# Weight buffers divided anew (eight raw, seven high, six low) and an instruction order worked out for loads that land later, in a two-layer hybrid attention block

## The chip, the cores and the metric

The kernel runs on one core of one Trainium2 chip. The metric is device time in microseconds of the whole program, and the time of the kernel before is the median of three runs. One more execution was profiled; every row below is of that one.

## The reference, cut to what matters

The reference runs a layer twice on x (256 tokens, width 1024), each time with weights of its own:

```python
def hybrid_layer(x, ...):
    hn = rms_norm(x, ln1)
    proj = hn @ w_in                      # 1024 x 2824: q, k, v of three mixers, and gates
    ...                                   # MoBA (6 heads), mLSTM (4 heads), sliding window (6 heads)
    x = x + jnp.concatenate([y_moba, y_mlstm, y_swa], axis=-1) @ w_out
    u = rms_norm(x, ln2) @ w_up           # 1024 x 4096
    return x + jnp.square(jax.nn.relu(u)) @ w_down
```

All of it is in float32. The small tensors of a layer (norm gains, convolution weights, sinks, gate biases) come to the kernel as one table per layer.

## The kernel before, in words

**Number format.** To keep float32 accuracy, the kernel splits each weight and each activation into a high and a low part and multiplies three times: high by high, high by low, low by high (`three`, L796; its matmuls are L798, L799 and L800). A split (`split`, L295) is one ScalarE copy that rounds to the high part (it shows as ACT L273, `whi<-raw`) and one VectorE subtraction for the low part (DVE L280, `wlo<-raw,whi`).

**How weights travel.** All weights are cut into units of at most 1040 columns by 128 rows (some 512 KB). A unit goes through three sets of buffers. `load_units` (L499) takes a raw buffer, and SyncE's queue loads the unit into it (SPq L300); it goes through the units strictly in the order of a list, so a load that waits for a buffer holds all later ones. `split_units` (L547) takes one high and one low buffer for each unit, again in the order of a list, and splits the raw one into them. TensorE reads the high and the low buffer; `used` (L334) gives them back after the last matmul. Before the change there are six raw, eight high and seven low buffers (`RAW`, `WHI`, `WLO`, L306 to L308).

**Stages of a layer.** The projections go through w_in in pieces of two or four row blocks, with attention (`pair`, `head`, `mlstm_pair`) between them. Then eight units of w_out are multiplied by four `mix` threads (L1387), each for 128 tokens and 512 columns, and each over all eight units; a unit is given back after the fourth. Then comes the feed-forward stage: 32 units of w_up (`up`, L1440: 24 matmuls of 256 columns each) and 32 row blocks of w_down, taken in pairs (`DownPair`, L368). Of a pair, sums of its quarters are made first: ScalarE copies a quarter out of the raw buffer (`first_sum`, L417), a DMA that adds in flight, issued on POOL (L422), adds another quarter to it, and VectorE makes the other sums (`first_sums`, `sums`, L397 and L426; DVE L280 on `arena` and `mids`). The pair then makes four parts, which `split_units` splits too, and `product` (L1482) multiplies them in seven products of three 512-column matmuls each. The sums need the raw buffers of both row blocks, so these are held longer than those of w_up. Meanwhile ScalarE and VectorE also square the results of `up` (`squared`, L1457) and split them (`fh`, `fl`).

**What sets the order.** Each engine executes its instructions in the order in which the program has them. That order is not written by hand: `Scheduler.run` (L165) simulates the engines while the program is built. Every step of every thread is an `Op` with an estimated duration; the scheduler takes the operation that can start first, and among nearly equal ones that of the lowest rank. For a DMA it adds the bytes at 330 GB/s, a latency of 2.2 us, and, from 60 us of its own clock on, `BUSY` = 0.8 us (L229):

```python
LATENCY = {"PE": 0.20, "ACT": 0.145, "DVE": 0.13, "POOL": 0.15, "DMA": 2.2}
...
            th.step(end + LATENCY[eng] + (BUSY if eng == "DMA" and end > 60 else 0))
```

These estimates decide only the order; on the chip, semaphores make each instruction wait until its inputs are really there. An operation whose input comes later than estimated therefore holds up everything behind it on its engine.

**The next layer's table.** `small_loads` (L648), a thread of rank 81 for layer 1, waits for the last use of layer 0's table (one tile holds both, L598), loads the table of the second layer (279 KB), and has VectorE make eight products from it, the rotary tables with the norm gains (`cg`, `sg`, L659), and `nsink`. The products are needed only in layer 1.

Of the kernel before, what the change touches and what calls it, by code (L numbers as in the profile page):

```python
# [11 lines left out]
F32R = mybir.dt.float32r  # L12
# [19 lines left out]
UNIT = 1040  # L32
# [96 lines left out]
LATENCY = {"PE": 0.20, "ACT": 0.145, "DVE": 0.13, "POOL": 0.15, "DMA": 2.2}  # L129
ISSUE = {"PE": 0.235, "ACT": 0.0, "DVE": 0.0, "POOL": 0.0, "DMA": 0.0}  # L130
SWITCH = 0.2
BUSY = 0.8
URGENTLY = -25
SOON = {"PE": 0.08, "ACT": 0.2, "DVE": 0.05, "POOL": 0.0, "DMA": 0.0}


class Scheduler:
# [27 lines left out]
    def run(self):  # L165
        while self.threads:
# [38 lines left out]
            if best is None:  # L205
                if not self.threads:
# [4 lines left out]
            t0, eng = best[0], best[1].engine  # L211
            t, th, op = min((c for c in ready if c[2].engine == eng and c[0] <= t0 + SOON[eng]),
                            key=lambda c: c[1].rank())
            if eng in ("ACT", "DVE") and op.cost > 0.3 and th.rank() > URGENTLY:

                soon = [c for c in ready if c[2].engine == eng and c[1].rank() <= URGENTLY
                        and t < c[0] < min(t + 0.3, t + op.cost - 0.3)]
# [9 lines left out]
            if op.bank:  # L227
                self.banks[op.bank] = eng, end + LATENCY[eng]
            th.step(end + LATENCY[eng] + (BUSY if eng == "DMA" and end > 60 else 0))  # L229

# [19 lines left out]
def tile_hybrid_block(ctx: ExitStack, tc: tile.TileContext, x, xT, smalls, w_in, w_out, w_up,  # L250
# [12 lines left out]
    def buffers(name, n, shape, dt=F32, pool=None):  # L263
        return Buffers([(pool or sb).tile(shape, dt, name=f"{name}{i}") for i in range(n)], name)
# [10 lines left out]
    def dve(waits, n, fn, rate=0.00104, pointers=(), bank=None):  # L275
        p = sum(isinstance(s, bass.AP) for s in pointers)
        return Op("DVE", n * rate + 0.068 + 0.065 * p, waits, fn, bank)
# [4 lines left out]
    def ts(waits, o, i, s1, s2, op0, op1=None, rate=0.00052):  # L282
        kw = {} if op1 is None else {"op1": op1}
        return dve(waits, free_size(o), lambda: V.tensor_scalar(o, i, s1, s2, op0=op0, **kw), rate, (s1, s2),
                   bank_of(i))
# [13 lines left out]
    def dma(waits, nbytes, o, i, eng=None):  # L299
        return Op("DMA", nbytes / 330e3, waits, lambda: (eng or nc.sync).dma_start(o, i))  # L300
# [2 lines left out]
    TMP = buffers("tmp", 5, [128, 512])  # L303
    mids = sb.tile([128, 10 * 384], F32, name="mids")
    MID = Buffers([mids[:, i * 384:i * 384 + 384] for i in range(10)], "mid")
    RAW = buffers("raw", 6, [128, UNIT])  # L306
    WHI = buffers("whi", 8, [128, UNIT], F32R)
    WLO = buffers("wlo", 7, [128, UNIT], F32R)  # L308
    FH = buffers("fh", 4, [128, 1024], F32R)
    FL = buffers("fl", 4, [128, 1024], F32R)  # L310

# [13 lines left out]
    class Unit:  # L325
# [7 lines left out]
        def used(self, t):  # L333
            self.uses -= 1  # L334
            in_use[0] = max(in_use[0], self.k + 1)
            if self.uses == 0:
                WHI.put(self.ih, t)
                WLO.put(self.il, t)

# [28 lines left out]
    class DownPair:  # L368
# [20 lines left out]
        def read(self, i, t):  # L389
# [4 lines left out]
            if not self.raws[i]:  # L394
                RAW.put(u.ir, u.t)

# [102 lines left out]
    def load_units():  # L499
        for k, u in enumerate(units):  # L500
# [9 lines left out]
            if k == 7:  # L510
                t = yield dma([], 262144, masks_t, masks)
                made.signal(t)
            u.ir, t = yield Get(RAW)
            u.raw = RAW.tiles[u.ir]
            dst = u.raw[:, :u.n].rearrange("p (k c) -> p k c", k=u.nk)
# [31 lines left out]
    def split_units():  # L547
        for k, u in enumerate(splits):
            u.k = k
            whole = isinstance(u, Part)  # L550
            yield Wait(*(u.ready if whole else [u.there]))
            u.ih, th = yield Get(WHI)
            u.il, tl = yield Get(WLO)
            h, lo = WHI.tiles[u.ih], WLO.tiles[u.il]
            raw = u.src() if whole else u.raw[:, :u.n]
# [8 lines left out]
            else:  # L564
                RAW.put(u.ir, t)
                u.hi = h[:, :u.n].rearrange("p (k c) -> p k c", k=u.nk)
# [33 lines left out]
    def table(l, a=0, b=T_END):  # L600
        return tab[l][:, a:b], smalls[l, :, a:b]
# [42 lines left out]
    tab_ev = [Event() for _ in range(DEPTH)]  # L644
# [3 lines left out]
    def small_loads(l, after):  # L648


        yield Wait(*after)
        if l:
            t = yield dma([], 300e3, *table(l))
            tab_ev[l].signal(t)
        g = tab[l][:, T_GB:T_SINK].rearrange("p (s i d) -> p s i d", s=2, i=4)
        t = max(e.t for e in (*after, tab_ev[l]))
        for k, o in enumerate((cg, sg)):
            for i in range(4):
                t = yield dve([t], 128, lambda k=k, o=o, i=i: V.scalar_tensor_tensor(  # L659
                    o[:, i], rope_t[:, k], -1.0 if i % 2 else HD ** -0.5,  # L660
                    g[:, k, i, None, :].to_broadcast([128, 2, HD]), op0=OP.mult, op1=OP.mult))
        t = yield ts([t], nsink, tab[l][:, T_SINK:T_BIAS], -1.0, None, OP.mult)
        small_ev[l].signal(t)
# [244 lines left out]
    class Layer:  # L908
# [703 lines left out]
        def start(self, base):  # L1612
# [59 lines left out]
            if l + 1 < DEPTH:  # L1672
                h2 = [e for b in range(2) for e in self.h2[b]]
                add(81, small_loads(l + 1, h2))
# [17 lines left out]
    sch.add(-9, load_units())  # L1692
    sch.add(50, split_units())
    sch.add(5, small_loads(0, x_ev[1]))
    L = None
    for l in range(DEPTH):
# [75 lines left out]
```

## Time and profile before

| what | us |
|---|---|
| median of three runs | 583.48 (582.37 to 585.88) |
| the profiled execution, its own time | 586.18 |
| its span, first to last instruction | 584.4 |
| TensorE busy in the span | 572.6 (98%) |
| VectorE busy | 541.9 (93%) |
| ScalarE busy | 433.7 (74%) |

How to read it: matmuls overlap, and their recorded ends are modelled, so a TensorE that shows as busy can still have waited; the time between the starts of two matmuls that follow each other tells. A number in brackets behind a row of the timeline is how long the engine stood idle before that row, and who ended it.

### The profile page before, as it was taken

How to read it: one execution, taken by the hardware profiler on the slowest of the kernel's cores; microseconds unless marked ns; L12 is line 12 of the kernel's file. 1: busy time of each engine (PE TensorE's matmuls, PEld its weight loads, DVE VectorE, ACT ScalarE, POOL GpSimd, SP SyncE). 2: the span in 40 equal slices, each digit the busy share in tenths (PEclk: the TensorE clock that was granted, in tenths of full speed). 3: DMA queues.
4: the chain of work that ended last, by engine and by line, in shares of the span. 5: the costliest groups of instructions: out<-in, count | busy, mean ns of one | idle time of the engine just before them, and what ended most of it. 6: DMA issues, size and time to landing. Idle time of an engine off the chain costs nothing.

```text
span 584.4 us, 10665 instructions
## 1 busy us (share of the span) xinstructions
PE 572.6 (98%) x3853; PEld 512.3 (88%) x3853; DVE 541.9 (93%) x1125; ACT 433.7 (74%) x835; POOL 34.3 (6%) x46
## 2 busy tenths in 40 slices
PE   8999999999999999999999999999999999999996
PEld 7999987798889999898689999877999898999884
DVE  6899999689899999999999999977999999999995
ACT  6966898676788776787676768967787786886860
POOL 4000000000010100101000000000100010100110
PEclk9999999999999999999999999999999999999999
DMA  9938346364877867776856353544767777777751
GB/s 317 356 92 229 102 135 190 110 208 120 248 222 206 265 193 234 227 214 190 262 153 175 96 186 109 169 157 144 204 175 237 231 191 216 243 207 227 230 113 72
DMA packets 45285, 111.83 MB, mean 191 GB/s; under 512 B 4048, under 2 KB 17616, under 8 KB 45232
## 3 DMA queue, kind: packets, MB, share of 16 engines
q1 hardware_dynamic: 40208, 102.21, 53.8%
q0 software_dynamic: 4736, 8.79, 9.7%
q8 instruction: 30, 0.49, 0.3%
q14 instruction: 23, 0.19, 0.1%
q10 hardware_dynamic: 288, 0.15, 0.1%
HBM read 110.08 MB, written 1.05 MB: 190 GB/s over the span
## 4 chain that ended last, share of the span: by engine, by line
PE 76%; DVE 9%; DMA 7%; ACT 3%; issue 3%; SPq 0%; DVEq 0%; ACTq 0%
PE ps L798 22%; PE ps L800 22%; PE ps L799 22%; DVE wlo L280 5%; DMA raw<-in_w_down_dram 4%; PE ps L875 2%; PE ps L1311 2%; PE ps L1329 2%; DVE arena L280 2%; PE ps L1500 1%; ACT whi L273 1%; DMA xs<-in_x_dram 1%; ACT arena L273 1%; DMA tab<-in_smalls_dram 1%; DVE xs L289 1%
## 5 line engine op out<-in xcount | busy, mean ns | idle before, releaser
L280 DVE TENSOR_TENSOR wlo<-raw,whi 128x512 fp32r<-128x512 f32 (+3 forms) x236 | 211.2, 916 | 8.1 <-ACT whi L273 7.2
L273 ACT ACTIVATE whi<-raw 128x512 fp32r<-128x512 f32 (+3 forms) x236 | 180.0, 807 | 1.7 <-DMA raw<-in_w_in_dram 1.5
L800 PE MATMUL ps<-hT,wlo 128*128 128x256 f32 x576 | 162.4, 282 | 3.2 <-DVE wlo L280 3.0
L798 PE MATMUL ps<-hT,whi 128*128 128x256 f32 x576 | 162.6, 282 | 0.8 <-ACT arena L273 0.4
L799 PE MATMUL ps<-lT,whi 128*128 128x256 f32 x576 | 161.8, 281 | 0.4 <-DVE lT L289 0.4
L798 PE MATMUL ps<-whi,fh 128*128 128x512 f32 x274 | 113.5, 414 | 0.0
L800 PEld LDWEIGHTS ps<-hT,wlo 128*128 128x128 f32 x576 | 108.7, 189 | 4.5 <-DVE wlo L280 4.5
L798 PEld LDWEIGHTS ps<-hT,whi 128*128 128x128 f32 x576 | 108.6, 189 | 2.8 <-ACT arena L273 0.8
L799 PEld LDWEIGHTS ps<-lT,whi 128*128 128x128 f32 x576 | 108.6, 189 | 1.8 <-DVE lT L289 0.6
L800 PE MATMUL ps<-whi,fl 128*128 128x512 f32 x274 | 107.8, 393 | 0.0
L799 PE MATMUL ps<-wlo,fh 128*128 128x512 f32 x274 | 107.7, 393 | 0.0
L798 PE MATMUL ps<-whi,hT 128*128 128x256 f32 (+2 forms) x256 | 80.2, 313 | 0.6 <-ACT whi L273 0.6
L799 PE MATMUL ps<-wlo,hT 128*128 128x256 f32 (+2 forms) x256 | 76.6, 299 | 0.6 <-DVE wlo L280 0.6
L800 PE MATMUL ps<-whi,lT 128*128 128x256 f32 (+2 forms) x256 | 76.3, 298 | 0.0
L798 PEld LDWEIGHTS ps<-whi,fh 128*128 128x128 f32 x274 | 51.5, 188 | 12.6 <-issue 3.3
L800 PEld LDWEIGHTS ps<-whi,fl 128*128 128x128 f32 x274 | 51.5, 188 | 11.9
L799 PEld LDWEIGHTS ps<-wlo,fh 128*128 128x128 f32 x274 | 51.6, 188 | 11.3 <-issue 2.2
L798 PEld LDWEIGHTS ps<-whi,hT 128*128 128x128 f32 x256 | 49.0, 191 | 3.3 <-issue 1.6
L799 PEld LDWEIGHTS ps<-wlo,hT 128*128 128x128 f32 x256 | 49.1, 192 | 1.6 <-DVE wlo L280 1.1
L800 PEld LDWEIGHTS ps<-whi,lT 128*128 128x128 f32 x256 | 48.9, 191 | 0.0
L273 ACT ACTIVATE arena<-ps 128x512 f32<-128x512 f32 (+3 forms) x52 | 26.2, 508 | 29.8 <-PE ps L800 27.5
L273 ACT ACTIVATE fh<-arena 128x1024 fp32r<-128x1024 f32 x30 | 31.8, 1059 | 16.6 <-DVE arena L280 15.5
(153 smaller groups left out, 816.4 us busy)
## 6 DMA issues: line engine op xcount, KB each, us to landing
raw<-in_w_up_dram SPq DMA_DIRECT2D x64, 512.0 KB, 4.7
raw<-in_w_down_dram SPq DMA_DIRECT2D x64, 512.0 KB, 4.6
raw<-in_w_in_dram SPq DMA_DIRECT2D x24, 512.0 KB, 4.6
raw<-in_w_out_dram SPq DMA_DIRECT2D x16, 512.0 KB, 3.4
raw<-in_w_in_dram SPq DMA_DIRECT2D x16, 384.0 KB, 3.7
arena<-in_w_down_dram POOLq DMA_DIRECT2D x20, 256.0 KB, 4.3
raw<-in_w_in_dram SPq DMA_DIRECT2D x7, 520.0 KB, 6.4
mids<-in_w_down_dram POOLq DMA_DIRECT2D x12, 256.0 KB, 4.3
```

Source lines behind the costliest of these rows:

```text
L273: lambda: A.activation(o, i, func, **kw), bank)
L280: return dve(waits, free_size(o), lambda: V.tensor_tensor(o, a, b, op=op), bank=bank_of(a, b))
L289: lambda: V.scalar_tensor_tensor(o, a, s, b, op0=op0, op1=op1), pointers=(s,),
L798: T.matmul(ps, s[0], m[0], start=start, stop=False)
L799: T.matmul(ps, s[0], m[1], start=False, stop=False)
L800: T.matmul(ps, s[1], m[0], start=False, stop=stop)
L875: T.transpose(ps[:, cs], src[:, cs], ident)
L1311: T.matmul(PS.tiles[ip][:, o], qT[b, i, q], kT[b, kc, k], start=o.start == 0, stop=o.start > 0)
L1329: T.matmul(yps[64 * n:64 * n + 64, o], vv[blk][:, d:d + HD], MID.tiles[pT[h]][:, cols], start=blk == 0, stop=blk == 1)
L1500: T.matmul(ps[:, c:d], self.rT[k][1][:, b], part.f[:, cols], start=k == 0, stop=end and d == 512)
```

## The change

The raw buffers become eight, the high ones seven and the low ones six; their sum stays 21, and all have the same size. `BUSY` goes from 0.8 to 1.5, so the scheduler believes that every load after 60 us of its clock lands 0.7 us later than it did. `LATER`, new, adds another 2.5 us to the time at which it believes the second layer's table to be there. No instruction is added or removed; which buffer each uses, and the order on each engine, follow from the scheduler's run with these numbers.

```diff
@@ -129,8 +129,9 @@
-BUSY = 0.8
+BUSY = 1.5
 URGENTLY = -25
+LATER = 2.5
@@ -303,9 +304,9 @@
-    RAW = buffers("raw", 6, [128, UNIT])
-    WHI = buffers("whi", 8, [128, UNIT], F32R)
-    WLO = buffers("wlo", 7, [128, UNIT], F32R)
+    RAW = buffers("raw", 8, [128, UNIT])
+    WHI = buffers("whi", 7, [128, UNIT], F32R)
+    WLO = buffers("wlo", 6, [128, UNIT], F32R)
@@ -651,7 +652,7 @@
             t = yield dma([], 300e3, *table(l))
-            tab_ev[l].signal(t)
+            tab_ev[l].signal(t + LATER)
```

## Rows read from the trace of the kernel before

**Rows 1.** The page's head and its first part.
```profile
span 584.4 us, 10665 instructions
...
PE 572.6 (98%) x3853; PEld 512.3 (88%) x3853; DVE 541.9 (93%) x1125; ACT 433.7 (74%) x835; POOL 34.3 (6%) x46
```

**Rows 2.** Sums by stretch (PE, PEld, DVE, ACT, POOL; clock, DMA), both feed-forward stages.
```profile
125.00:285.00 160.00, 157.15 (x1030) 142.71 (x1029) 151.95 (x209) 118.64 (x150) 13.11 (x16) 1.00 0.75 221
...
413.00:570.00 157.00, 155.89 (x1034) 142.31 (x1033) 151.18 (x200) 118.10 (x148) 12.90 (x15) 1.00 0.73 208
```

**Rows 3.** Timeline of TensorE: neighbouring matmuls with a late start, layer 0.
```profile
142.27 0.28 PE L799 MATMUL ps<-lT,whi 128*128 128x256 f32 x1
143.99 0.39 PE L800 MATMUL ps<-hT,wlo 128*128 128x256 f32 x1 [1.44 <-DVE wlo L280]
...
152.02 0.39 PE L800 MATMUL ps<-whi,fl 128*128 128x512 f32 x1
152.81 0.39 PE L798 MATMUL ps<-hT,whi 128*128 128x256 f32 x1 [0.40 <-ACT arena L273]
...
164.87 0.28 PE L798 MATMUL ps<-hT,whi 128*128 128x256 f32 x1
164.99 0.28 PE L799 MATMUL ps<-lT,whi 128*128 128x256 f32 x1
165.85 0.39 PE L800 MATMUL ps<-hT,wlo 128*128 128x256 f32 x1 [0.58 <-DVE wlo L280]
```

**Rows 4.** The same of layer 1.
```profile
490.07 0.40 PE L799 MATMUL ps<-wlo,fh 128*128 128x512 f32 x1
490.31 0.39 PE L800 MATMUL ps<-whi,fl 128*128 128x512 f32 x1
491.05 0.38 PE L798 MATMUL ps<-hT,whi 128*128 128x256 f32 x1 [0.35 <-ACT whi L273]
491.27 0.28 PE L799 MATMUL ps<-lT,whi 128*128 128x256 f32 x1
492.31 0.39 PE L800 MATMUL ps<-hT,wlo 128*128 128x256 f32 x1 [0.76 <-DVE wlo L280]
```

**Rows 5.** The chain that ended last (start, duration): the second layer's table.
```profile
124.59 6.30 DMA tab<-in_smalls_dram
```

**Rows 6.** Timeline of VectorE: the first product made from that table.
```profile
130.92 0.29 DVE L659 SCALAR_TENSOR_TENSOR cg<-rope_t,tab 128x128 f32<-128x128 f32 x1 [2.25 <-DMA tab<-in_smalls_dram]
```

**Rows 7.** Waits of SyncE's queue, feed-forward of layer 0 (in total, times, longest).
```profile
SPq L300 <- DVE wlo L280: 99.0, 49, 10.4
```

**Rows 8.** Timeline of ScalarE: copies of a w_down quarter, layers 0 and 1.
```profile
151.64 0.63 ACT L273 ACTIVATE mids<-raw 128x512 f32<-128x512 f32 x1 [2.55 <-DMA raw<-in_w_down_dram]
...
488.26 0.63 ACT L273 ACTIVATE arena<-raw 128x512 f32<-128x512 f32 x1 [3.62 <-DMA raw<-in_w_down_dram]
```

**Rows 9.** Waits of VectorE, feed-forward of layer 0 and, below the dots, of layer 1.
```profile
DVE arena L280 <- ACT arena L273: 3.6, 6, 1.3
DVE mids L280 <- DMA raw<-in_w_down_dram: 0.8, 2, 0.7
...
DVE arena L280 <- ACT arena L273: 3.1, 6, 1.1
DVE arena L280 <- DMA raw<-in_w_down_dram: 1.2, 2, 0.8
```

**Rows 10.** Timeline of VectorE, layer 1: low parts of w_out units, the first, seventh and eighth.
```profile
372.11 1.22 DVE L280 TENSOR_TENSOR wlo<-raw,whi 128x1024 fp32r<-128x1024 f32 x1
...
386.27 1.20 DVE L280 TENSOR_TENSOR wlo<-raw,whi 128x1024 fp32r<-128x1024 f32 x1
...
399.22 2.36 DVE L280 TENSOR_TENSOR wlo<-raw,whi 128x1024 fp32r<-128x1024 f32 x2 [3.16 <-ACT whi L273]
```

**Rows 11.** Timeline of TensorE there: `mix`, seventh unit's first read, fourth thread's first unit.
```profile
393.65 0.40 PE L799 MATMUL ps<-wlo,fh 128*128 128x512 f32 x1
...
397.79 0.40 PE L799 MATMUL ps<-wlo,fh 128*128 128x512 f32 x1
```

## The prediction

> **What bounds the kernel now.** I read the page's first part, then the sums by stage, then TensorE's timeline, and only then the waits. The page shows TensorE busy for 98% of the span and VectorE for 93% [rows 1]. The sums by stage say where that is tight: in the two feed-forward stages, 160 and 157 us long, TensorE is busy for 157.15 and 155.89 us, and VectorE for 151.95 and 151.18, that is 95 and 96% [rows 2]. Two engines are nearly full there, and VectorE feeds TensorE. The clock is 1.00 throughout, so it plays no part.
>
> Since recorded ends of matmuls are modelled, I go by starts. Where nothing is missing, a 256-column matmul starts 0.12 us after the one before it (164.87 to 164.99 [rows 3]), and one after a 512-column matmul 0.24 us (490.07 to 490.31 [rows 4]). What exceeds this is waiting. In layer 0: 143.99 - 142.27 - 0.12 = 1.60, 152.81 - 152.02 - 0.24 = 0.55, 165.85 - 164.99 - 0.12 = 0.74, together 2.89 us [rows 3]. In layer 1: 0.74 - 0.24 = 0.50 and 1.04 - 0.12 = 0.92, together 1.42 us [rows 4]. These five hold 4.31 us; the timeline has three more in layer 0, all under 0.4 us, which I don't count. Whatever a better order may do, it has little more than 4.3 us of TensorE's waiting to take in these stages; the matmuls stay as they are.
>
> Two causes lie behind them. First, the second layer's table is issued at 124.59 and takes 6.30 us [rows 5]; VectorE's next instruction in order is made from it, and so VectorE stands for 2.25 us in mid-stage [rows 6], though layer 1 is far away. The chain that ended last goes from this landing on through VectorE, almost without a break, until 143; the 1.60 us at 143.99 come out of it. Second, raw buffers: in layer 0's stage SyncE waits 99.0 us in 49 waits for VectorE to finish with a raw buffer [rows 7], so each load starts only when the sixth-last unit is done with. ScalarE, which copies a quarter of a w_down row block, arrives before its load: 2.55 us of standing at 151.64, 3.62 at 488.26 [rows 8]. VectorE's sums wait for these copies: 3.6 us in six waits in layer 0 and 3.1 in layer 1, with 0.8 and 1.2 us straight for the load [rows 9]. An engine that is 95% busy doesn't catch up quickly; TensorE's waits at 152.81, 165.85, 491.05 and 492.31 follow such a stand.
>
> **The change part by part.** No instruction comes or goes, so every term is a wait or a shift.
>
> *Table, `LATER` and `BUSY`.* The scheduler reckoned 300 KB at 330 GB/s (0.91 us), 2.2 and 0.8: the table was due 3.9 us after its issue, and came after 6.3. Now it reckons 3.9 + 0.7 + 2.5 = 7.1 us. The products go behind other VectorE work, of which there is enough (95% busy), and are needed only a hundred microseconds later. VectorE regains 2.25 us; TensorE regains the 1.60. What moves: eight products and `nsink` on VectorE, some 3 us later; the transfer itself and SyncE's order stay unless the raw loads around it move. Bounds: 0 if the freed time only brings the next wait nearer, 1.60 if all is given on. I take 1.6, since the stretch from 130.92 to 143 is almost all VectorE work.
>
> *Raw from six to eight.* Each load starts two units earlier. The stage passes 64 units in some 160 us [rows 2], 2.5 us each, so loads start 5 us sooner. ScalarE's stands of 2.55 and 3.62 us are shorter than that [rows 8], so the copies stop waiting. Of the remaining 2.71 us (0.55 + 0.74 + 1.42) I take 2.3; the rest I leave to coincidence, since the low parts for `up` come late for other reasons too. Bounds: 0 and 2.71. It costs no more transfers; earlier loads only share the queue sooner, at a DMA share of 0.75 [rows 2]. The new order also shifts instructions that I cannot see; for that I add 0.3 us, with bounds of 1.5 us to either side (about the largest single wait that the order before made, 1.60).
>
> *`BUSY` for the other loads.* In the order, work on a load moves 0.7 us back, while on the chip it is there 5 us sooner. Cost nothing: the 5 us cover it, without them it would be 0.7 us of lookahead.
>
> *High from eight to seven, low from seven to six.* Where this binds can be seen at one place. In layer 1 the first seven w_out units are split from 372.11 to 386.27, and the eighth only at 399.22 [rows 10], because no unit is released before the fourth `mix` thread has read it, which begins just before 397.79 [rows 11]. With six low buffers the seventh unit too must wait. It is first read at 393.65; from there to 397.79 three threads use it, 3 products of 3 x 0.23 = 0.7 us, 2.1 us in all. Upper bound: these 2.1 us of TensorE have nothing in their place. Lower bound 0: the scheduler puts the fourth thread, which has been waiting only for its rank, into the gap, and that releases the first unit 3 us sooner. I take 0, because by the code that thread lacks nothing but rank once it has a PSUM bank; that a bank is free there is an assumption. If that cover is missing, 2.1 us. In layer 0 the same units are further apart, and I take 0 there as well. In the feed-forward stages VectorE has no wait ended by TensorE, hence none for a low buffer [rows 9]; I take 0 and put the upper bound into the second rival.
>
> Sum: -1.6 - 2.3 + 0.3 = -3.6 us, so the profiled execution's 586.18 (a span of 584.4 and 1.8 around it) would become 582.6. It lies 2.7 above the median of 583.48. If the 2.7 are of another kind, the median becomes 583.48 - 3.6 = 579.9. If they are the same late landings, the median run holds only 4.3 - 2.7 = 1.6 of them, and 582 remains. I take the middle, 580.8.
>
> **Rivals.** *VectorE is the bound, and its work is the same.* It is 151.95 of 160 us busy in the stage, and its remaining 8.05 us are idle in small pieces [rows 2]. If what is freed is idled away elsewhere by the same unevenness, the time stays: 583.5, give or take 1. For it: both engines are full. Against it: TensorE's five waits each follow a stand of VectorE or ScalarE. The Trainium skill ("Perfetto Trace Analysis", section Identifying the Most-Contended Engine) has TensorE judged by the busy share of its weight loads and not by its matmuls; by that TensorE would stand at 142.71 of 160, 89%, below VectorE's 95%, and this rival would be the forecast. The starts say otherwise: between the waits no matmul is late, so I keep it second.
>
> *Fewer split buffers make VectorE wait (the other side).* VectorE works ahead of TensorE until low buffers run out. With one less it stops a unit earlier; each block of four `up` units and two pairs would then cost it a wait of up to two products, 1.4 us, in the seven inner blocks of a layer: 10 us. Freed are 2.25 + 3.6 + 0.8 = 6.7 us of VectorE in layer 0 and 4.3 in layer 1 [rows 6, 9]. VectorE would need 160 - 6.7 + 10 = 163.3 and 157 - 4.3 + 10 = 162.7 us: +3.3 and +5.7, 592.5 from the median. It decides from 6.7 us a layer on in layer 0, 4.3 in layer 1; with half of the 10 it is about even, and at three quarters +0.8 and +3.2, 587.5. For it: the seven buffers are all full at the w_out units [rows 10]. Against it: no wait of this kind today.
>
> *The change does only half of what it says:* the table's stand goes, the w_down waits stay, since the sums need other buffers too: -1.6, 582.
>
> **How the numbers follow.** Forecast 0.55 (579 to 582.3), half of it 0.17 (near 582), no change 0.14 (582.5 to 584.5), slower 0.14 (584.5 to 592.5, half of that above 588). A measurement of this kernel can tell about 1% from no change, 5.8 us here. Faster by more than that needs more than all counted waits and luck with the order (577.6 or less): 0.07. Slower by more (589.3 or more) is the upper half of the second rival: 0.07. The rest, 0.86, lies within 1%. For 8 in 10 I go from 577.8 (the forecast's 579.9 with the order's 1.5 and a little on the good side) to 586 (into the slower rival).
>
> **What would show it.** Right: no VectorE idle time before `cg`; ScalarE's waits for `raw<-in_w_down_dram` near zero; TensorE's gaps at the `up` units gone, the feed-forward stages some 2.5 and 1.3 us shorter; SyncE still waiting for raw buffers, with loads landing 5 us before use. The seventh w_out unit split late and the fourth `mix` thread begun earlier, without a gap. Wrong: VectorE waits ended by TensorE before `wlo`, TensorE gaps in front of `mix`, or feed-forward stages as long as before with VectorE at 95%.

## The result, and the profile after

| | before | after |
|---|---|---|
| median, nine runs each on one chip (us) | 583.48 (581.97 to 586.12) | 580.95 (580.10 to 582.55) |
| ratio, 95% interval | | 0.9949 [0.9929, 0.9969] |
| the profiled execution, its own time | 586.18 | 581.00 |
| its span | 584.4 | 579.2 |

The change takes half a per cent off, less than the 1% that was taken for the limit of what can be told, but with 1 outside the interval. The profiled executions lie 5.2 us apart and the medians only 2.5: the execution profiled before was a long one, that after a middling one.

The page of the kernel after, head, first part and three rows of the DMA issues (count, KB each, median us from issue to landing):

```profile
span 579.2 us, 10694 instructions
...
PE 570.7 (99%) x3853; PEld 511.7 (88%) x3853; DVE 543.8 (94%) x1130; ACT 431.1 (74%) x830; POOL 34.3 (6%) x46
...
raw<-in_w_up_dram SPq DMA_DIRECT2D x64, 512.0 KB, 4.2
...
raw<-in_w_down_dram SPq DMA_DIRECT2D x64, 512.0 KB, 5.1
...
arena<-in_w_down_dram POOLq DMA_DIRECT2D x20, 256.0 KB, 5.5
```

The same number of matmuls as in [rows 1] fills a shorter span. VectorE has five instructions more than there, and ScalarE five fewer: for a few multiplications in the attention the program leaves the choice of the engine to the scheduler (`either`), and it gave five more of them to VectorE. The section on the change and the prediction left this out. They lie outside the feed-forward stages; VectorE's busy time grew by 1.9 us over the span. Sums by stretch for the two feed-forward stages, columns as in [rows 2]:

```profile
125.00:282.50 157.50, 156.47 (x1034) 142.67 (x1033) 153.62 (x212) 121.19 (x154) 12.86 (x15) 1.00 0.75 225
...
408.50:565.00 156.50, 156.50 (x1043) 143.30 (x1042) 152.77 (x203) 119.27 (x151) 12.91 (x15) 1.00 0.69 207
```

VectorE is now busy for 153.62 of 157.50 us and 152.77 of 156.50, 97.5 and 97.6%; of its idle time 3.9 and 3.7 us remain, where [rows 2] left 8.05 and 5.82. Taken exactly, from the first `up` matmul of a layer to the first of its last w_down products, those with unsplit operands (L1500, L1501 after): in layer 0 from 119.46 to 285.03 before and from 119.87 to 282.52 after, 2.9 us less; in layer 1 from 407.88 to 570.18 and from 404.31 to 565.00, 1.6 less. These 4.5 of the span's 5.2 us are the stages that the prediction named.

TensorE's waits between 110 and 600 us (in total, times, longest), of the kernel before:

```profile
PE ps L800 <- DVE wlo L280: 3.0, 4, 1.4
PE ps L740 <- DVE xs L289: 0.4, 1, 0.4
PE ps L799 <- DVE lT L289: 0.4, 1, 0.4
PE ps L798 <- ACT arena L273: 0.4, 1, 0.4
PE ps L798 <- ACT whi L273: 0.4, 1, 0.4
```

and of the kernel after:

```profile
PE ps L801 <- DVE wlo L281: 0.9, 2, 0.6
```

**The table.** SyncE's queue just before the table, POOL's transfer there, and the table's time to land, before:

```profile
121.51 1.57 SPq L300 DMA_DIRECT2D raw<-in_w_up_dram  x2
...
124.33 0.91 POOL L422 DMA_DIRECT2D arena<-in_w_down_dram  x1 [116.16 <-ACT arena L273]
...
124.59 0.33 SPq L300 DMA_DIRECT2D tab<-in_smalls_dram  x1
...
DMA to landing us min/median/max: 6.3/6.3/6.3
```

and after:

```profile
113.08 1.93 SPq L301 DMA_DIRECT2D raw<-in_w_up_dram  x2
...
120.14 0.91 POOL L423 DMA_DIRECT2D arena<-in_w_down_dram  x1 [111.97 <-PE ps L801]
...
124.07 0.33 SPq L301 DMA_DIRECT2D tab<-in_smalls_dram  x1
...
DMA to landing us min/median/max: 2.8/2.8/2.8
```

VectorE's timeline after shows the products without a stand in front of them, where [rows 6] had 2.25 us:

```profile
127.61 1.81 DVE L281 TENSOR_TENSOR wlo<-raw,whi 128x1024 fp32r<-128x1024 f32 x2
129.34 0.89 DVE L660 SCALAR_TENSOR_TENSOR cg<-rope_t,tab 128x128 f32<-128x128 f32 x4
```

But look at the landing. With six raw buffers two w_up loads of 512 KB were issued 2 and 3 us ahead of the table and an adding transfer of 256 KB 0.3 us ahead, and it took 6.3 us. With eight, the loads had gone out 9 and 11 us ahead and the adding transfer 4, and it landed in 2.8, sooner than even the 3.9 us of the old estimates. `LATER` covers a lateness that was no longer there.

**The w_down loads.** ScalarE's waits for w_down in the whole program before:

```profile
ACT arena L273 <- DMA raw<-in_w_down_dram: 16.3, 7, 4.4
ACT mids L273 <- DMA raw<-in_w_down_dram: 16.3, 8, 3.5
```

ScalarE's waits in layer 0's stage after, then VectorE's, then SyncE's:

```profile
ACT arena L274 <- PE ps L801: 31.1, 15, 2.8
ACT mids L274 <- DMA raw<-in_w_down_dram: 1.8, 2, 1.6
ACT arena L274 <- DMA raw<-in_w_down_dram: 0.2, 1, 0.2
...
DVE arena L281 <- ACT arena L274: 1.7, 3, 0.6
...
SPq L301 <- DVE wlo L281: 106.9, 51, 6.3
SPq L301 <- DVE arena L281: 23.1, 6, 8.1
```

ScalarE waits for w_down for 2.0 us, and in layer 1 not at all; before it was 32.6 us in the whole program. It now waits for TensorE instead, which delays no matmul here. SyncE still waits for raw buffers: with the waits that end with one of VectorE's sums (23.1 us here, 33.1 before) it is 130.0 us, against 132.1 before, where [rows 7] shows the first part alone. One wait is left that goes all the way from a load through ScalarE and VectorE to TensorE (timelines of the three):

```profile
184.10 0.63 ACT L274 ACTIVATE mids<-raw 128x512 f32<-128x512 f32 x1 [1.65 <-DMA raw<-in_w_down_dram]
...
185.72 1.22 DVE L281 TENSOR_TENSOR wlo<-raw,whi 128x1024 fp32r<-128x1024 f32 x1 [1.42 <-ACT whi L274]
...
194.02 0.28 PE L800 MATMUL ps<-lT,whi 128*128 128x256 f32 x1
194.94 0.38 PE L801 MATMUL ps<-hT,wlo 128*128 128x256 f32 x1 [0.64 <-DVE wlo L281]
```

By the starts that matmul is 0.92 - 0.12 = 0.80 us late. So loads do not all land 5 us before their use. TensorE's other wait in this stage is what is left near the place where [rows 3] had 1.60 us, now 0.58 - 0.12 = 0.46:

```profile
142.57 0.28 PE L800 MATMUL ps<-lT,whi 128*128 128x256 f32 x1
143.15 0.39 PE L801 MATMUL ps<-hT,wlo 128*128 128x256 f32 x1 [0.30 <-DVE wlo L281]
```

**The w_out units of layer 1.** VectorE's low parts, first, sixth, and seventh with eighth, and TensorE's first read by the fourth `mix` thread:

```profile
369.41 1.22 DVE L281 TENSOR_TENSOR wlo<-raw,whi 128x1024 fp32r<-128x1024 f32 x1
...
381.27 1.22 DVE L281 TENSOR_TENSOR wlo<-raw,whi 128x1024 fp32r<-128x1024 f32 x1
...
394.50 2.36 DVE L281 TENSOR_TENSOR wlo<-raw,whi 128x1024 fp32r<-128x1024 f32 x2 [2.50 <-ACT whi L274]
...
393.00 0.40 PE L800 MATMUL ps<-wlo,fh 128*128 128x512 f32 x1
```

Six units are split ahead instead of seven, and the fourth thread begins 24 us after the first split, at 393.00, where in [rows 10, 11] it was 26 us. It filled the gap: TensorE has no wait there.

### The profile page after: what moved, and what is told of

Same layout as the page of the kernel before. It is cut to its first block, busy times and chain, and to the rows that moved or that the text cites. A ratio compares the mean times of both kernels' runs of the same rounds, so it can differ in the third digit from the quotient of the medians.

```text
span 579.2 us, 10694 instructions
## 1 busy us (share of the span) xinstructions
PE 570.7 (99%) x3853; PEld 511.7 (88%) x3853; DVE 543.8 (94%) x1130; ACT 431.1 (74%) x830; POOL 34.3 (6%) x46
## 4 chain that ended last, share of the span: by engine, by line
PE 88%; DMA 5%; DVE 4%; issue 1%; ACT 1%; SPq 0%; DVEq 0%; ACTq 0%
PE ps L799 26%; PE ps L801 26%; PE ps L800 26%; PE ps L876 2%; DMA raw<-in_w_in_dram 2%; PE ps L1312 2%; PE ps L1330 2%; PE ps L1501 2%; DVE wlo L281 2%; DMA raw<-in_w_down_dram 1%; DMA mids<-in_xT_dram 1%; DVE arena L281 1%; DVE xs L290 1%; PE ps L771 1%; DMA tab<-in_smalls_dram 1%
## 5 line engine op out<-in xcount | busy, mean ns | idle before, releaser
L281 DVE TENSOR_TENSOR wlo<-arena,whi 128x1024 fp32r<-128x1024 f32 x36 | 43.2, 1217 | 0.0
```

The source lines that it names most:

```text
L281: return dve(waits, free_size(o), lambda: V.tensor_tensor(o, a, b, op=op), bank=bank_of(a, b))
```

## The experiments

Each ratio is against the kernel before on the same chip. Kernels of one group shared its runs (before: 584.28 us, 25 runs, in the first; 585.07, 29, in the second; 583.71, 21, in the third; 585.69, 12, in the last). "Eight raw" stands for eight raw, seven high, six low buffers.

### One part at a time

**Buffers alone.**

```diff
-    RAW = buffers("raw", 6, [128, UNIT])
-    WHI = buffers("whi", 8, [128, UNIT], F32R)
-    WLO = buffers("wlo", 7, [128, UNIT], F32R)
+    RAW = buffers("raw", 8, [128, UNIT])
+    WHI = buffers("whi", 7, [128, UNIT], F32R)
+    WLO = buffers("wlo", 6, [128, UNIT], F32R)
```

> Only the buffers change (eight raw, seven high, six low); BUSY 0.8 and no LATER. Theory (earlier loads end the waits for w_down, the table's wait is a term of its own): ScalarE's waits for raw w_down loads fall from 32.6 us to under 8, VectorE still stands some 2.2 us before the first product from the table; 0.7 to 2 us faster than before, 581.5 to 582.8. Rival 1 (the estimates make the gain, the buffers none): 583.5 within 0.7. Rival 2 (fewer split buffers make VectorE wait): 584.5 or more, with VectorE waits before wlo that TensorE ends.

579.45 us, ratio 0.9922 [0.9903, 0.9941], below the theory's range. One part alone gives all that the whole change gives, and a little more. The table takes 3.0 us without `LATER`; TensorE's waits between 110 and 600 us are gone altogether. Yet ScalarE still waits for w_down, 7.7 us (its waits over the whole program):

```profile
ACT arena L274 <- DMA raw<-in_w_down_dram: 6.0, 4, 2.8
ACT mids L274 <- DMA raw<-in_w_down_dram: 1.7, 2, 1.3
```

**`LATER` alone.**

```diff
+LATER = 2.5
-            tab_ev[l].signal(t)
+            tab_ev[l].signal(t + LATER)
```

> Only LATER = 2.5; BUSY 0.8 and buffers six, eight, seven. Theory: VectorE's wait before the first product from the table falls from 2.25 us to under 0.5, the TensorE wait of 1.60 us near 144 goes, the w_down waits stay near 30 us; 0.7 to 1.6 us faster, 581.9 to 582.8. Rival 1 (freed time is idled away by the next wait): 583.5 within 0.5 although the table's wait is gone.

582.40, ratio 0.9963 [0.9940, 0.9986]. Here, with six raw buffers, `LATER` does what it says: the table takes 6.5 us, and the first product does not wait. The w_down waits stay as they were before, 30 us:

```profile
131.89 0.29 DVE L660 SCALAR_TENSOR_TENSOR cg<-rope_t,tab 128x128 f32<-128x128 f32 x1
...
ACT arena L274 <- DMA raw<-in_w_down_dram: 16.3, 8, 3.1
...
ACT mids L274 <- DMA raw<-in_w_down_dram: 13.6, 8, 2.8
```

**`BUSY` alone.**

```diff
-BUSY = 0.8
+BUSY = 1.5
```

> Only BUSY = 1.5; no LATER, buffers six, eight, seven. Theory: the table's wait falls by 0.7 of its 2.25 us, the waits for w_down loads fall a little, since work on them is put 0.7 us back; 0 to 1 us faster, 582.5 to 583.5. Rival 1 (the estimates make the gain): 581 to 582. Rival 3 (any new order gives as much): between 580.5 and 586 with no relation to the waits.

581.25, ratio 0.9951 [0.9930, 0.9972], below the theory's range too. With six raw buffers still, ScalarE's w_down waits sink to 1.4 us; nothing but the order differs, so a later estimate can end the same waits as an earlier load. The ratio is that of the whole change (0.9949): by itself this number gave as much, on the old buffers.

**Both estimates, old buffers.** `BUSY = 1.5` and `LATER = 2.5`.

> Both estimates (BUSY 1.5, LATER 2.5), buffers six, eight, seven. Theory: the table's wait is gone, the w_down waits are smaller but there (over 15 us on ScalarE); 1 to 2 us faster, 581.5 to 582.5, so above the changed kernel's 580.95 by what the raw buffers give. Rival 1 (the estimates make the gain, the buffers none): 581.0 within 0.5.

582.98, ratio 0.9987 [0.9965, 1.0009]: not to be told from no change, and above the theory's range. The two gains don't add. Each number makes another order of the whole program, and what one order gains the next may lose.

### Is it the earlier load or the other order?

More raw buffers change two things: loads really start sooner, and the scheduler, which knows of the buffers, makes another order. To part them I kept the high and low buffers at seven and six and gave the scheduler six raw ones in both of the next kernels. In the second, eight tiles lie behind them: the time at which a buffer is believed free comes from the six, but the tile is the one that has been idle longest. The last three lines of the edit are what parts the two kernels. Every engine's order of instructions is then the same; only the waits for a raw buffer end sooner.

```diff
+class Spread(Buffers):
+    def __init__(self, tiles, known, name=""):
+        self.name, self.tiles = name, tiles
+        self.free = [(0.0, i) for i in range(known)]
+        self.idle = list(range(len(tiles)))
+    def take(self):
+        t, i = min(self.free)
+        self.free.remove((t, i))
+        return self.idle.pop(0), t
...
-    RAW = buffers("raw", 6, [128, UNIT])
+    RAW = buffers("raw", 8, [128, UNIT])
     RAW = Spread(RAW.tiles, 6, "raw")
```

Six known, six there:

> Six raw, seven high, six low buffers, BUSY 0.8, no LATER: one high and one low buffer fewer than before and nothing given for them. Theory: the low buffers cost nearly nothing, 583 to 585, and the w_down waits stay near 30 us on ScalarE. Rival 2 (fewer split buffers make VectorE wait): 586 or more, with VectorE waits before wlo that TensorE ends, in the feed-forward stages.

Six known, eight there:

> Every engine has the same instructions in the same order as in the run with six, seven and six; only the raw tiles rotate through eight instead of six, which the scheduler isn't told. So the one thing that changes on the chip is that loads may start two units earlier. Theory: loads land some 5 us earlier before use, ScalarE's waits for w_down fall from about 30 us to under 5, and it is 1.5 to 3 us faster than the run with six raw tiles. Rival 3 (the gain comes from the new order, not from the loads): within 0.5 us of it.

586.11, ratio 1.0037 [1.0008, 1.0065], and 584.42, ratio 1.0007 [0.9979, 1.0035]. Three things follow.

First, with six raw buffers and one high and one low buffer less the kernel is slower by 0.37%, about 2 us. The time lies in the second rival's range, but its path doesn't show: VectorE has no wait ended by TensorE before a low part, nor ScalarE one before a high part. It is one order only; whether the two buffers cost this, or the order that they happen to make, stays open.

Second, the earlier loads by themselves give 1.7 us. The table shows them at work: in the same order, it lands in 3.0 us in place of 4.2, for the w_up load ahead of it now goes out at 113.18 and not at 121.82. ScalarE's waits over the program with six there

```profile
ACT arena L292 <- DMA raw<-in_w_down_dram: 17.3, 7, 3.7
...
ACT mids L292 <- DMA raw<-in_w_down_dram: 16.0, 9, 3.2
```

are 33.3 us for w_down; with eight there no such line is left. From a w_down load's landing to the first instruction that waits for it pass 1.3 us in the median with six tiles there and 6.3 with eight (loads of the feed-forward stages), the 5 us that the prediction had. And the time is still that of the kernel before. So ScalarE's stand was not what held most of the time up: 33 us of waits removed, 1.7 us gained.

Third, from here to the buffers alone (579.45), where the same eight tiles are known to the scheduler, it is another 0.85% (0.9922 / 1.0007), 5 us, give or take 2 by the two intervals: in this pair the larger part is the order. Its loads do not land sooner before their use: there it is 1.3 us again. What the order for six does wrong shows in the timelines of TensorE and VectorE around 534 and 555 us, with eight tiles there:

```profile
534.02 0.28 PE L819 MATMUL ps<-lT,whi 128*128 128x256 f32 x1
534.38 0.39 PE L820 MATMUL ps<-hT,wlo 128*128 128x256 f32 x1
...
553.98 0.40 PE L818 MATMUL ps<-whi,fh 128*128 128x512 f32 x1
555.32 0.50 PE L819 MATMUL ps<-wlo,fh 128*128 128x512 f32 x1 [0.94 <-DVE wlo L299]
...
531.97 1.22 DVE L299 TENSOR_TENSOR fl<-arena,fh 128x1024 fp32r<-128x1024 f32 x1
533.11 1.22 DVE L299 TENSOR_TENSOR wlo<-raw,whi 128x1024 fp32r<-128x1024 f32 x1
...
552.91 1.22 DVE L299 TENSOR_TENSOR fl<-arena,fh 128x1024 fp32r<-128x1024 f32 x1
554.05 1.22 DVE L299 TENSOR_TENSOR wlo<-mids,whi 128x1024 fp32r<-128x1024 f32 x1
```

TensorE starts 0.36 - 0.12 = 0.24 us late at 534.38 and 1.34 - 0.24 = 1.10 at 555.32. At 534.38 VectorE has no idle time just before: it makes the low part of `fh` (531.97) ahead of that of the `up` unit (533.11), which TensorE wants next. This comes back in nine blocks of the two stages, some 21.4 us apart, each time 0.24 to 0.28 us, 2.3 in all. The buffers alone, with the same eight tiles, have the two the other way round,

```profile
527.36 1.22 DVE L281 TENSOR_TENSOR wlo<-raw,whi 128x1024 fp32r<-128x1024 f32 x1
528.50 1.22 DVE L281 TENSOR_TENSOR fl<-arena,fh 128x1024 fp32r<-128x1024 f32 x1
```

and no matmul there is late: a wrong sequence, not a late input. The 1.10 us at 555.32 stand behind `fl` (552.91) in the same way, though VectorE had also stood for 1.0 us in two waits for ScalarE some 6 to 10 us earlier, so its cause is not shown as clearly. The rest of the 5 us is spread too thin to be laid to single places.

**The change without `LATER`**, that is eight raw and `BUSY = 1.5`.

> The changed kernel without LATER (BUSY 1.5, buffers eight, seven, six). Theory: VectorE stands about 1.5 us before the first product from the table, and TensorE waits 0.5 to 1.5 us more some 10 us later; 581.5 to 582.5. Rival 1 (freed time is idled away anyway, so the table is worth nothing): 581.0 within 0.4.

579.78, ratio 0.9931 [0.9905, 0.9957]. The theory missed: without `LATER` the result stays, and the table's wait doesn't come back.

### Is it luck with one order?

Every number gives another order, so one pair proves little. Four kernels move `BUSY` by a little, 0.7 and 0.9 in place of 0.8, without `LATER`, two with each set of buffers.

```diff
-BUSY = 0.8
+BUSY = 0.7        # in the other two: 0.9; each with six raw (6, 8, 7) and with eight raw (8, 7, 6)
```

Six raw, 0.7:

> The kernel before with BUSY 0.7 in place of 0.8: a new order that nobody chose, six raw buffers. Theory (the raw buffers matter, the order scatters around it): somewhere in 581 to 586, the w_down waits of ScalarE over 15 us or VectorE late in another way. Rival 3 (any new order gains as much as the change): 581.5 or less, as low as with eight raw buffers.

Six raw, 0.9:

> The kernel before with BUSY 0.9: another order with six raw buffers. Theory: 581 to 586, above both runs with eight. Rival 3: 581.5 or less.

Eight raw, 0.7:

> Eight, seven, six buffers with BUSY 0.7 and no LATER. Theory: as the run with 0.8 (579.45), 579 to 581, below both runs with six raw buffers. Rival 3: as far scattered as with six, 580 to 586.

Eight raw, 0.9:

> Eight, seven, six buffers with BUSY 0.9 and no LATER. Theory: 579 to 581, with the table landing some 3 us after its issue and VectorE not waiting for it. Rival 3: 580 to 586.

Measured, in this sequence: 584.69, ratio 1.0014 [0.9985, 1.0042]; 582.52, 0.9964 [0.9938, 0.9990]; 579.35, 0.9901 [0.9869, 0.9933]; 579.28, 0.9904 [0.9871, 0.9936]. The gain is not that of one lucky order: both orders for eight lie below both for six. With six raw the ratio sinks as `BUSY` rises, 1.0014, 1, 0.9964, 0.9951 at 0.7, 0.8, 0.9 and 1.5; with eight it is flat, 0.9901, 0.9922, 0.9904, 0.9931. The table's stand is there with six raw at 0.7 and 0.9 (landing in 6.1 and 6.2 us), of which this is the second,

```profile
131.28 0.29 DVE L660 SCALAR_TENSOR_TENSOR cg<-rope_t,tab 128x128 f32<-128x128 f32 x1 [2.18 <-DMA tab<-in_smalls_dram]
```

and with eight at neither. Six raw buffers don't always bring it: with `BUSY` alone the table landed in 4.1 us, with six known and six there in 4.2, and VectorE did not stand in either.

**Eight raw with `LATER`, `BUSY` at 0.8.** This asks whether `LATER` is what keeps the changed kernel above the buffers alone. The edit, shortened, against the kernel before:

```diff
+LATER = 2.5
-    RAW, WHI, WLO = 6, 8, 7
+    RAW, WHI, WLO = 8, 7, 6
```

> Eight, seven, six buffers and LATER = 2.5 with BUSY 0.8: against the run with these buffers alone (579.45) only LATER is added. With eight raw buffers the table lands about 3 us after its issue, so LATER covers a lateness that is gone. Theory: LATER gives nothing here, 579 to 580.2. If LATER itself costs what the changed kernel lies above the same kernel without it (580.95 against 579.78): 580.4 to 581.2.

579.83, ratio 0.9910 [0.9872, 0.9948]. `LATER` by itself neither helps nor harms beside eight raw buffers.

All six orders for eight raw buffers have ratios from 0.9901 to 0.9949, all that know six from 0.9951 to 1.0037; the nearest two, the whole change and `BUSY` alone, can't be told apart. In the mean the six ratios of the eight-raw kernels are 0.9920; those of the six kernels with the old buffers, the one before with 1 among them, are 0.9980. The gain of the buffers over orders of all kinds is thus 0.60%, 3.5 us, of which 1.7 are earlier loads if these are worth as much in other orders as in the one where they were measured, and some 1.8 the order (an estimate, since no second pair parts the two); that is less than the 5 us of the pair above, whose order was the slowest of all.

The best that was run are the buffers alone, with `BUSY` at 0.7 to 0.9, some 0.8 to 1.0% below the kernel before. The changed kernel is the highest of the eight-raw ones, by about 1 us; the intervals overlap, and whether `BUSY` and `LATER` together cost that is open.

## Why the prediction was right or wrong

**The bound.** Right. The time came out of TensorE's waits in the two feed-forward stages: 2.9 and 1.6 us, where 2.5 and 1.3 had been forecast. Of the 4.31 us of late starts counted from [rows 3, 4] two waits are left, 0.46 and 0.80.

**The median.** 580.95 against 580.8, in the range. The sum of -3.6 us was meant for the profiled execution, and that fell by 5.2. The middle between the two ways of carrying it to the median made up for it: the second of these ways has it that this execution was long because it held more of what the change removes. That fits, but no other execution of the kernel before was traced, so the nearness of the median is in part luck.

**Table, `LATER` and `BUSY`: -1.6.** The wait went, and this step named the wrong part. It took it that the table would go on landing after 6.3 us with work moved in front of its products. It lands in 2.8 us, and the two w_up loads ahead of it go out sooner; that the one makes the other is best seen where the order is held fixed (4.2 us with six tiles, 3.0 with eight). The step's own remark, that the transfer stays unless the raw loads around it move, was the point to follow up: they moved by 8 us. `LATER` was seen to work as described only with six raw buffers.

**Raw from six to eight: -2.3.** The size was about right for the two stages, the mechanism only in part. ScalarE's waits did all but vanish, 32.6 to 2.0 us. But the run with six known and eight there takes all of them away for 1.7 us, and the buffers alone keep 7.7 of such waits and are 5 us faster than that. "Loads start 5 us sooner" held in the order as it was; the new order spends most of the lead again. From a w_down load's landing to its first use pass 1.8 us in the median in the changed kernel and 1.4 in the one before, against 6.3 where the scheduler wasn't told of the tiles; the wait of 1.65 us at 184.10 is of that kind.

**The reorder: +0.3, bounds 1.5 to either side.** This is the step that failed. It treated the new order as noise of either sign. It has a direction: an order made with eight raw buffers in mind was worth 5 us (give or take 2) in the pair where it alone differed, about three times the bound, and by the estimate above some 1.8 in the mean over orders. The forecast came out near all the same because the step before it had claimed for the loads most of what the order gave; that the two misses cancel is luck.

**`BUSY` for the other loads: 0.** Held with eight raw buffers (ratio 0.9922 without it, 0.9931 with it). The reason given, that the earlier loads cover it, is not shown, for the new order spends their lead; with six it was worth 0.49%, where the prediction had it at nothing or 0.7 us of lookahead.

**High and low buffers: 0.** At the w_out units it went as predicted: six units split ahead, the fourth `mix` thread sooner, no gap. Whether it is nothing in sum is open: +0.37% in the one order with six raw buffers; with eight it was not run apart.

**The rivals.** "VectorE is the bound" would have left 583.5, and it fell: in layer 0's stage VectorE had 8 us of idle time to give, and gave half. The Trainium skill ("Perfetto Trace Analysis", section Identifying the Most-Contended Engine), by whose share of weight loads VectorE stood above TensorE, would put it there in the kernel after as well: 97.5% busy against 142.67 of 157.50 us, 91%, for the weight loads. This case's starts say otherwise in both kernels: with two matmuls left that are late by 0.4 us or more, 1.26 us together, TensorE is the bound, and VectorE, with under 4 us of idle time, is close behind. "Fewer split buffers make VectorE wait" fell too: no VectorE wait before a low part ends with TensorE, no ScalarE wait before a high part does, and the kernel that had the fewer buffers alone lost 2 us where this rival reckoned with up to 9. "Half of what it says" would have kept the w_down waits; they went.

## What to carry to other kernels

Where a program orders its instructions by simulated resources, a buffer more may be worth as much through the better order as through the earlier transfer; to part the two, keep the order and change only the tiles behind it. Correct an estimate only after the buffers are settled: the lateness that it describes belongs to the old queue, and here it was gone with two more buffers. And count a wait only by what reaches the bounding engine: 33 us of ScalarE's standing were worth 1.7 in the order where they were taken away.

## What the hardware showed that I had not expected

The time that the 279 KB table takes to land goes with what was issued just ahead of it. With two 512 KB loads 2 and 3 us ahead on its queue and POOL's 256 KB 0.3 us ahead, six kernels had it in 6.3 us (before), 6.5, 4.1, 5.8, 6.1 and 6.2; with one w_up load 2.4 us ahead 4.2; with one w_down load 2.1 us ahead, in four kernels, or none within 9 us, in three, 2.8 to 3.0. Why one of the six, `BUSY` alone, had only 4.1 was not found, and the shares of the two queues are not parted.

The spread of a kernel's runs goes with its raw buffers. With the order held fixed, twelve runs each spread over 3.2 us (585.45 to 588.63) with six tiles and over 1.1 us (583.76 to 584.84) with eight. The other six-raw kernels spread over 4.0 to 5.2 us (the kernel before, in its groups of 12 to 29 runs, over 7.4 to 8.3), the eight-raw ones over 1.1 to 2.5, from 5 to 12 runs each. It would fit that landings differ from run to run and that a deeper set of buffers absorbs the late ones; of each kernel only one execution was traced, so this is not shown.

Finally, single transfers did not all get faster with the smaller waits: w_down loads took 5.1 us in the median where the kernel before had 4.6, and POOL's adding transfers into `arena` 5.5 in place of 4.3, but w_up loads 4.2 in place of 4.7.
